# Seven-product units stored with their sums, and SBUF moved from GpSimd's descriptor room to buffers

## The chip, the cores and the metric

The kernel runs on one core of one Trainium2 chip. TensorE does the matrix products, VectorE (DVE), ScalarE (ACT) and GpSimd (POOL) the elementwise work, and SyncE (SP) issues most of the DMA transfers. The metric is the device time of one execution in microseconds (us). Of several runs the median is taken.

## The reference

Two layers of a decoder trunk, on 256 rows of 2048 columns in float32. The part around the change is the MLP:

```python
for l in range(DEPTH):                       # DEPTH = 2
    h = _rmsnorm(x, attn_norm_g[l])
    ...                                      # attention, gated convolution
    x = x + jnp.concatenate([attn, conv], axis=-1) @ w_out[l]
    hm = _rmsnorm(x, mlp_norm_g[l]) @ w_up[l]            # 2048 -> 8192
    x = x + jnp.square(jax.nn.relu(hm)) @ w_down[l]      # 8192 -> 2048
```

## The kernel before, in words

**Precision.** Every float32 operand is cut into two parts of type float32r, a high one (an ACT copy) and the rest (a VectorE subtraction). A product is then three matmuls: high by high, high by low, low by high. So each weight tile costs ACT and VectorE one instruction each (`halves`, lines 291 and 292; `column`, lines 719 and 720).

**The MLP of a layer** (`mlp`, from line 693) has a left and a right half.

*Left half.* A loop runs over 32 pairs of hidden blocks (a pair is 256 hidden columns). For pair i, `up_part` multiplies the normed activations (`nT`) with two columns of w_up, each in two passes `kh`; `evict` adds the two parts into a tile `h` of [128, 8, 128]; `square` applies relu, a scaling by the ratio of the two row tiles' norms (`mnorm.ratio`, made by the matmul at line 462), and the square. Planes 0 to 3 of `h` are the four 128x128 blocks A11, A21, A12, A22 of the pair: two row tiles by two hidden blocks. Planes 4 to 7 are sums S1 to S4 of them. `in_forms` makes these sums with four VectorE additions (lines 890 to 893) and cuts all eight planes into `f` (lines 895 and 896). Two pairs later (LAG) the pair's `f` meets the left 1024 columns of w_down in seven products instead of eight (Strassen's scheme), whose weight operands are four quarters and four sums of quarters (`quarters`: `b1`, `b2`, `t`, `t13`, `t24`, from a tile `draw`). Seven PSUM banks gather these products over the pairs. The last two pairs are multiplied plainly (line 985).

*Right half.* The same pairs meet the right 1024 columns of w_down. Twelve of them (SEVEN: 4, 6, 8, 11, ... 28) are again done with seven products, the twenty others (PLAIN) with eight (line 1060). What they need was stored in DRAM during the left half by GpSimd's DMA queue: of a plain pair the cut planes 0 to 3 (`plain`, line 883, two pairs to a tensor), of a unit the four squared planes in float32 (`hid`, line 879). In the right half `block(b)` loads two plain pairs in one transfer into a tile `g` (line 955, GpSimd's queue; the four tiles are shared with `nT`), and `load_again` loads a unit into a tile `h` (line 806, SyncE's queue); `unit` then runs `in_forms` on it, sums and cuts, and asks for the next unit. Matmuls of the right half write to banks named `rt`.

**Buffers.** `h` has one tile, `f` two; `draw` two; `uraw` (columns of w_up, and rows of w_down of plain pairs in the right half) three; `t24` one. GpSimd's DMA descriptors have 16384 bytes of each partition, the default.

**What sets the order.** TensorE's instructions run in program order. Those of the other engines and the DMA queues are ordered when the kernel is built, by a planner that simulates a time line; each engine then runs its own list in that order and waits where an operand or a buffer is missing. Weight cuts are listed as jobs: `weights.take()` makes them three ahead of use (AHEAD), in an order written out in `weights.order`, in which the four jobs of a unit (plain quarters, sums, the unit's `f`, further sums) stand between the rows of the plain pairs ahead of it. Small pieces of background work (`work.start`, `work.tick`) are put between the matmuls, a piece's `yield n` being n ticks; in `up_part` a tick stands after every four matmuls. `factors` is the piece that makes the row norms and, for the MLP, the ratio matmul.

**The first pair** (i = 0) runs its two columns side by side: both use one PSUM tile `up0` of two banks, in the order first pass of column 0, first pass of column 1, second pass of column 0 with its eviction, second pass of column 1 with its eviction.

## Time and profile before

| | us |
|---|---|
| three runs | 2167.89, 2167.99, 2170.19 |
| median | 2167.99 |
| profiled execution | 2165.76 |
| its span | 2164.0 |

The profile is of one execution. Its page gives busy times by engine, DMA queues, and the chain of work that ended last. By that chain 85% of the span is TensorE, 7% VectorE, 4% DMA. The mean granted clock of TensorE was 0.998. The stages in the span, by the chain: the mixer of layer 0 until about 395 us, its MLP until about 1090 us (right half from 912), the mixer of layer 1 until about 1469, its MLP to the end (right half from about 1985). In rows of the timeline the columns are start, duration, engine, line, operation, tiles and shapes, and in brackets the idle time before it with what ended it. A DMA row's time in the chain is from its issue to its landing.

### The profile page before, as it was taken

How to read it: one execution, taken by the hardware profiler on the slowest of the kernel's cores; microseconds unless marked ns; L12 is line 12 of the kernel's file. 1: busy time of each engine (PE TensorE's matmuls, PEld its weight loads, DVE VectorE, ACT ScalarE, POOL GpSimd, SP SyncE). 2: the span in 40 equal slices, each digit the busy share in tenths (PEclk: the TensorE clock that was granted, in tenths of full speed). 3: DMA queues.
4: the chain of work that ended last, by engine and by line, in shares of the span. 5: the costliest groups of instructions: out<-in, count | busy, mean ns of one | idle time of the engine just before them, and what ended most of it. 6: DMA issues, size and time to landing. Idle time of an engine off the chain costs nothing.

```text
span 2164.0 us, 29108 instructions
## 1 busy us (share of the span) xinstructions
PE 2136.1 (99%) x10966; PEld 1812.7 (84%) x10966; DVE 1710.8 (79%) x2397; ACT 1300.9 (60%) x1760; POOL 166.2 (8%) x246
## 2 busy tenths in 40 slices
PE   9999999999999999999999999999999999999999
PEld 7888888888888888788788888888888888887877
DVE  5677655698888888799866776557988888887997
ACT  6556445566666666656565664446666666665554
POOL 3021200000000000000001222000000000000000
PEclk9999999999999999999999999999999999999999
DMA  7655766587767777887565557656777767778873
GB/s 256 183 158 166 236 187 188 160 263 217 227 216 231 224 224 223 272 288 275 188 184 176 156 166 245 186 172 196 253 227 219 224 216 232 222 224 274 310 271 108
DMA packets 285534, 467.62 MB, mean 216 GB/s; under 512 B 10611, under 2 KB 191429, under 8 KB 282832
## 3 DMA queue, kind: packets, MB, share of 16 engines
q1 hardware_dynamic: 268128, 413.17, 61.2%
q0 software_dynamic: 17216, 52.56, 7.0%
q8 instruction: 86, 1.41, 0.3%
q14 instruction: 56, 0.46, 0.1%
q10 hardware_dynamic: 48, 0.02, 0.0%
HBM read 436.32 MB, written 29.38 MB: 215 GB/s over the span
## 4 chain that ended last, share of the span: by engine, by line
PE 85%; DVE 7%; DMA 4%; issue 2%; ACT 1%; POOL 1%; DVEq 0%; POOLq 0%; ACTq 0%
PE upc L856 30%; PE pr L904 13%; PE o L361 8%; PE rt L1060 5%; PE gb L383 4%; PE v L361 4%; PE ci L383 4%; PE gc L383 4%; PE rt L904 3%; PE q L361 3%; PE k L361 3%; DVE wlo L292 2%; DMA draw<-in_w_down_dram 1%; DMA h<-hid 1%; PE upw L856 1%
## 5 line engine op out<-in xcount | busy, mean ns | idle before, releaser
L291 ACT ACTIVATE whi<-raw 128x1024 fp32r<-128x1024 f32 (+1 forms) x338 | 355.6, 1054 | 410.6 <-PE rt L1060 87.8
L292 DVE TENSOR_TENSOR wlo<-raw,whi 128x1024 fp32r<-128x1024 f32 (+1 forms) x338 | 414.4, 1229 | 237.3 <-ACT whi L291 232.7
L856 PE MATMUL upc<-nT,uhi 128*128 128x512 f32 x1920 | 477.6, 391 | 0.0
L719 ACT ACTIVATE uhi<-uraw 128x1024 fp32r<-128x1024 f32 x256 | 271.2, 1060 | 288.1 <-PE upc L856 254.2
L856 PEld LDWEIGHTS upc<-nT,uhi 128*128 128x128 f32 x1920 | 352.8, 188 | 68.2
L720 DVE TENSOR_TENSOR ulo<-uraw,uhi 128x1024 fp32r<-128x1024 f32 x256 | 313.0, 1223 | 115.7 <-ACT uhi L719 113.3
L856 PEld LDWEIGHTS upc<-nT,ulo 128*128 128x128 f32 x1920 | 261.9, 190 | 18.7
L856 PE MATMUL upc<-nT,ulo 128*128 128x256 f32 x1920 | 267.7, 282 | 0.0
L1060 PE MATMUL rt<-whi,g 128*128 128x512 f32 x608 | 194.0, 393 | 0.0
L361 PE MATMUL o<-whi,cat 128*128 128x512 f32 x512 | 159.6, 390 | 0.0
L1060 PEld LDWEIGHTS rt<-whi,g 128*128 128x128 f32 x608 | 115.7, 190 | 24.1
L1060 PE MATMUL rt<-wlo,g 128*128 128x512 f32 x304 | 120.3, 396 | 9.4 <-DVE wlo L292 9.2
L361 PEld LDWEIGHTS o<-whi,cat 128*128 128x128 f32 x512 | 96.1, 188 | 19.7
L754 DVE TENSOR_TENSOR t<-draw 128x1024 f32<-128x1024 f32 x84 | 102.4, 1219 | 11.0 <-DMA draw<-in_w_down_dram 10.8
L740 ACT ACTIVATE b2h<-draw 128x1024 fp32r<-128x1024 f32 x84 | 88.9, 1058 | 34.6 <-PE pr L904 25.9
L896 DVE TENSOR_TENSOR f<-h,f 128x1024 fp32r<-128x1024 f32 (+1 forms) x88 | 105.2, 1196 | 0.2 <-ACT f L895 0.2
L741 DVE TENSOR_TENSOR t13l<-t,t13h 128x1024 fp32r<-128x1024 f32 x84 | 102.8, 1224 | 2.0 <-ACT t13h L740 0.5
L741 DVE TENSOR_TENSOR t24l<-t,t24h 128x1024 fp32r<-128x1024 f32 x84 | 102.4, 1219 | 0.6 <-ACT t24h L740 0.2
L741 DVE TENSOR_TENSOR b2l<-draw,b2h 128x1024 fp32r<-128x1024 f32 x84 | 102.4, 1219 | 0.4 <-ACT b2h L740 0.3
L361 PE MATMUL o<-wlo,cat 128*128 128x512 f32 x256 | 99.6, 389 | 0.0
L895 ACT ACTIVATE f<-h 128x1024 fp32r<-128x1024 f32 (+1 forms) x88 | 90.4, 1027 | 9.4 <-DVE h L893 9.2
L740 ACT ACTIVATE t24h<-t 128x1024 fp32r<-128x1024 f32 x84 | 88.4, 1052 | 9.6 <-DVE t L758 6.4
(359 smaller groups left out, 3841.9 us busy)
## 6 DMA issues: line engine op xcount, KB each, us to landing
uraw<-in_w_up_dram SPq DMA_DIRECT2D x128, 1024.0 KB, 6.5
raw<-in_w_in_dram SPq DMA_DIRECT2D x191, 512.0 KB, 4.0
draw<-in_w_down_dram SPq DMA_DIRECT2D x88, 1024.0 KB, 5.4
raw<-in_w_down_dram SPq DMA_DIRECT2D x40, 1024.0 KB, 5.6
raw<-in_w_out_dram SPq DMA_DIRECT2D x64, 512.0 KB, 3.6
plain<-f POOLq DMA_DIRECT2D x40, 512.0 KB, 6.5
g<-plain POOLq DMA_DIRECT2D x20, 1024.0 KB, 8.3
hid<-h POOLq DMA_DIRECT2D x24, 256.0 KB, 5.5
```

The source lines that it names most:

```text
L291: a = nc.scalar.activation(hi[:, k], raw[:, k], AF.Copy)
L292: d = nc.vector.tensor_sub(lo[:, k], raw[:, k], hi[:, k].bitcast(F32))
L361: nc.tensor.matmul(acc[:, t], a.ap[:, pa, k % KG, t * P:(t + 1) * P], (hi, lo)[pw][:, j], start=(k == 0 and n == 0), stop=(k == nk - 1 and ...
L383: nc.tensor.matmul(acc[:, f, 0] if part else acc[:, f], wt[:, k % 4, fs], a.ap[:, 0, k % KG] if part else a.ap[:, :, k % KG], start=(part ...
L719: nc.scalar.activation(hi, src, AF.Copy)
L720: nc.vector.tensor_sub(lo, src, hi.bitcast(F32))
L740: keep(nc.scalar.activation(hi, src, AF.Copy))
L741: keep(nc.vector.tensor_sub(lo, src, hi.bitcast(F32)))
L856: nc.tensor.matmul(acc[:, 0] if part else acc, wt[:, k], a.ap[:, 0, k % KG] if part else a.ap[:, :, k % KG], start=(part == 0 and kh == 0 ...
L896: nc.vector.tensor_sub(f[:, 1, :n], h[:, :n], f[:, 0, :n].bitcast(F32))
L904: nc.tensor.matmul(prods[n], f[:, pa, a], b[pw], start=(start and m == 0), stop=(stop and m == 2))
L1060: nc.tensor.matmul(prods[p], blocks[b][:, slot, pa, 2 * k + t], w[pw][:, n], start=(i == PLAIN[0] and k == 0 and m == 0), stop=False)
```

## The change

It does these things:

- The sums S1 to S4 of a unit are made before the pair is stored, and `hid` keeps seven planes (all but A21, which no product uses by itself) instead of four. In the right half a unit is only loaded and cut, seven planes wide (`rounded`), with no additions.
- So that the seven planes lie side by side, A11 and A21 change places, and A12 and A22: the roles of the two row tiles are exchanged, in the products' outputs too.
- `h` gets two tiles instead of one, `draw` three instead of two, `t24` two instead of one. GpSimd's descriptor room goes from 16384 to 4096 bytes per partition.
- A block is loaded in two transfers, one for each of its pairs. Block 1 and the first unit are asked for inside the right half's loop instead of ahead of it, the later blocks one plain pair later than before.
- The first pair's two columns get a PSUM tile each.
- The ratio matmul of the MLP's norm comes after nine ticks instead of five.

```diff
-                yield 5
+                yield 9
                 tp = bank("rbc")
...
-    A11, A21, A12, A22, S1, S2, S3, S4 = range(8)
+    A21, A11, A22, A12, S1, S2, S3, S4 = range(8)
...
-            dpool = scope.enter_context(tc.tile_pool(name="dpool", bufs=2))
+            dpool = scope.enter_context(tc.tile_pool(name="dpool", bufs=3))
...
-                    h, lw = parts(forms["t"][:, 2:4], "t24", 1)
+                    h, lw = parts(forms["t"][:, 2:4], "t24", 2)
...
-            hid = {i: dram.tile([P, 4 * P], F32, name=f"hid{l}_{i}") for i in SEVEN}
+            hid = {i: dram.tile([P, 7 * P], F32, name=f"hid{l}_{i}") for i in SEVEN}
...
             def load_again(i):
-                again[i] = fpool.tile([P, 8, P], F32, tag="h", name="h", bufs=1)
-                nc.sync.dma_start(again[i][:, :4].rearrange("p a c -> p (a c)"), hid[i])
+                again[i] = fpool.tile([P, 8, P], F32, tag="h", name="h", bufs=2)
+                nc.sync.dma_start(again[i][:, 1:].rearrange("p a c -> p (a c)"), hid[i])
...
-                    f = in_forms(again[i], True)
+                    f = rounded(again[i], 1, 8)
...
-                if i in hid:
-                    nc.gpsimd.dma_start(hid[i], u)
-                f = in_forms(h, i < NP - LAG)
...
+                if i < NP - LAG:
                     nc.vector.tensor_add(h[:, S1], h[:, A21], h[:, A22])
                     nc.vector.tensor_sub(h[:, S2], h[:, S1], h[:, A11])
                     nc.vector.tensor_sub(h[:, S3], h[:, A11], h[:, A21])
                     nc.vector.tensor_sub(h[:, S4], h[:, A12], h[:, S2])
+                if i in hid:
+                    nc.gpsimd.dma_start(hid[i], h[:, 1:].rearrange("p a c -> p (a c)"))
+                    return rounded(h, 1, 8)
+                f = rounded(h, 0, 8 if i < NP - LAG else 4)
+                b = PLAIN.index(i)
+                nc.gpsimd.dma_start(plain[b // 2][:, b % 2], f[:, :, :4])
+                return f
+
+            def rounded(h, lo, hi):
                 f = fpool.tile([P, 2, 8, P], F32R, tag="f", name="f")
-                nc.scalar.activation(f[:, 0, :n], h[:, :n], AF.Copy)
-                nc.vector.tensor_sub(f[:, 1, :n], h[:, :n], f[:, 0, :n].bitcast(F32))
+                nc.scalar.activation(f[:, 0, lo:hi], h[:, lo:hi], AF.Copy)
+                nc.vector.tensor_sub(f[:, 1, lo:hi], h[:, lo:hi], f[:, 0, lo:hi].bitcast(F32))
                 return f
...
-                h = fpool.tile([P, 8, P], F32, tag="h", name="h", bufs=1)
+                h = fpool.tile([P, 8, P], F32, tag="h", name="h", bufs=2)
                 if i == 0:
-                    two = mm.tile([P, 2, CH], F32, tag="mm2", name="up0")
-                    two = [two[:, c].rearrange("p (h s) -> p h s", h=2) for c in range(2)]
+                    two = [mm.tile([P, 2, CH], F32, tag="mm2", name=f"up{c}")[:, 0].rearrange(
+                        "p (h s) -> p h s", h=2) for c in range(2)]
...
             def block(b):
                 blocks[b] = apool.tile([P, 2, 2, 4, P], F32R, tag="a", name="g")
-                nc.gpsimd.dma_start(blocks[b], plain[b])
+                for s in range(2):
+                    nc.gpsimd.dma_start(blocks[b][:, s], plain[b][:, s])
 
             block(0)
-            block(1)
-            load_again(SEVEN[0])
...
-            OWN = ((0, 0, 2), (0, 1, 4), (1, 0, 3), (1, 1, 8))
-            left = [xs[n][:, t] for n in range(2) for t in range(NT)]
-            right = [xs[2 + n][:, t] for n in range(2) for t in range(NT)]
+            OWN = ((0, 1, 2), (0, 0, 4), (1, 1, 3), (1, 0, 8))
+            left = [xs[n][:, t] for n in range(2) for t in (1, 0)]
+            right = [xs[2 + n][:, t] for n in range(2) for t in (1, 0)]
...
-                if slot == 0 and b + 2 < len(plain):
+                if slot == 0 and b == 0:
+                    block(1)
+                if slot == 1 and b + 2 < len(plain):
                     block(b + 2)
+                if slot == 1 and b == 0:
+                    load_again(SEVEN[0])
...
-    nc = _bacc.Bacc("TRN2", target_bir_lowering=False, num_devices=1)
+    nc = _bacc.Bacc("TRN2", target_bir_lowering=False, num_devices=1,
+                    dynamic_dma_scratch_size=4096)
```

More of the change, by code (lines that the diff above doesn't have):

```diff
@@ L877, in square @@
                 nc.scalar.activation(u, u, AF.Square)
-                if i in hid:
-                    nc.gpsimd.dma_start(hid[i], u)
-                f = in_forms(h, i < NP - LAG)
-                if i not in hid:
-                    b = PLAIN.index(i)
-                    nc.gpsimd.dma_start(plain[b // 2][:, b % 2], f[:, :, :4])
-                return f
-            def in_forms(h, sums):
-                n = 4
-                if sums:
-                    n = 8
+                if i < NP - LAG:
                     nc.vector.tensor_add(h[:, S1], h[:, A21], h[:, A22])
```

## The prediction

> **What bounds the kernel now.** I read the page first, then sums over stretches of time, then the timeline of TensorE for every place where it sat idle, and last the chain of waits at those places. The page:

> ```profile
> span 2164.0 us, 29108 instructions
> PE 2136.1 (99%) x10966; PEld 1812.7 (84%) x10966; DVE 1710.8 (79%) x2397; ACT 1300.9 (60%) x1760; POOL 166.2 (8%) x246
> ```

> TensorE is busy for all but 28 us. The change alters no matmul count, so it can only take idle time away, or add some. Two stretches in the body of the MLP (us, then busy time of PE, PEld, DVE, ACT, POOL, then clock, DMA share, GB/s), the first from the columns of w_up, the second from the right half of w_down:

> ```profile
> 438.83:885.72 446.89, 446.42 (x2382) 385.64 (x2381) 399.25 (x539) 300.44 (x365) 18.97 (x29) 1.00 0.74 227
> 951.54:1022.94 71.40, 71.40 (x316) 59.14 (x316) 69.79 (x91) 45.74 (x48) 2.12 (x4) 1.00 0.79 275
> ```

> Both bodies are full. In the second VectorE has only 1.6 us to spare in 71.4 us, that is in seven periods of 10.2 us (one seven-product pair and one plain pair). So what there is to win lies at the borders. The timeline of TensorE, with the idle time and its releaser in brackets, shows these waits in the MLP of layer 0 (first six) and of layer 1 (last six):

> ```profile
> 402.44 0.46 PE L462 MATMUL rbc<-diag,ones 128*128 128x128 f32 x2 [0.53 <-DVE diag L459]
> 407.75 0.49 PE L856 MATMUL up<-nT,uhi 128*128 128x512 f32 x1 [1.57 <-ACT ev L866]
> 477.20 0.50 PE L904 MATMUL pr<-b1h,f 128*128 128x512 f32 x1 [0.47 <-DVE f L896]
> 914.38 0.50 PE L1060 MATMUL rt<-wlo,g 128*128 128x512 f32 x1 [1.62 <-DVE wlo L292]
> 920.25 0.50 PE L1060 MATMUL rt<-wlo,g 128*128 128x512 f32 x1 [2.81 <-DVE wlo L292]
> 1056.43 0.50 PE L904 MATMUL rt<-b1h,f 128*128 128x512 f32 x1 [1.76 <-DVE f L896]
> ...
> 1476.35 0.46 PE L462 MATMUL rbc<-diag,ones 128*128 128x128 f32 x2 [0.53 <-DVE diag L459]
> 1480.77 1.42 PE L856 MATMUL up<-nT,uhi 128*128 128x512 f32 x5 [0.69 <-ACT ev L866]
> 1549.69 0.50 PE L904 MATMUL pr<-b1h,f 128*128 128x512 f32 x1 [0.47 <-DVE f L896]
> 1987.23 0.50 PE L1060 MATMUL rt<-wlo,g 128*128 128x512 f32 x1 [1.98 <-DVE wlo L292]
> 1993.10 0.80 PE L1060 MATMUL rt<-wlo,g 128*128 128x512 f32 x1 [2.81 <-DVE wlo L292]
> 2092.99 0.50 PE L904 MATMUL rt<-b1h,f 128*128 128x512 f32 x1 [1.50 <-DVE f L896]
> ```

> They add up to 16.7 us. Nearly all of them are in code that the diff touches.

> **Part by part.**

> *The ratio matmul (yield 5 to 9).* It is put four ticks later, from inside the third of the four first column passes to its end. Its input is ready 0.53 us after TensorE now asks for it, and a tick is four matmuls, so the wait goes in both layers: 1.1 us. It moves past no DMA, and its reader, the scaling of the first pair, comes only after the second half is copied out.

> *Two PSUM tiles for the first pair.* Now both column halves share one tile, and the last pass of the second half waits until ACT has copied out the first: 1.57 and 0.69 us. With a tile each this wait is gone. What is late next? In layer 0 ACT stood before that copy at a weight cut, behind this load (chain of waits):

> ```profile
> 395.61 10.46 DMA uraw<-in_w_up_dram
> ```

> It landed at 406.07, and the passes that need those weights come after the second half's last pass, so they are covered. But TensorE now comes some 2 us earlier into the first products, where VectorE is behind. Bounds 0 and 2.3 us; I take 1.6, nearer the whole, since the cuts there are released by TensorE and move with it. The second tile takes the buffer of the last output projection, whose two additions the transposes ahead of it wait for anyway: nothing.

> *Two h tiles.* The first pairs' f comes 0.47 us late in both layers, since a pair's eviction waits until the f before it is made. Bounds 0 and 0.9 us, I take 0.6: VectorE is nearly full there.

> *The start of the right half.* This is the largest term. TensorE waits for wlo, and VectorE, which makes it, had itself waited (first the chain of waits, then GpSimd, SyncE and VectorE in the timeline):

> ```profile
> 898.23 13.72 DMA draw<-in_w_down_dram
> 1970.72 14.07 DMA draw<-in_w_down_dram
> ...
> 896.62 1.12 POOL L955 DMA_DIRECT2D g<-plain  x2 [5.05 <-PE upc L856]
> 899.41 1.06 POOL L955 DMA_DIRECT2D g<-plain  x2 [1.67 <-PE upc L856]
> 905.43 0.34 SPq L806 DMA_DIRECT2D h<-hid  x1
> 911.97 1.23 DVE L754 TENSOR_TENSOR t<-draw 128x1024 f32<-128x1024 f32 x1 [5.23 <-DMA draw<-in_w_down_dram]
> 1984.82 1.22 DVE L754 TENSOR_TENSOR t<-draw 128x1024 f32<-128x1024 f32 x1 [5.59 <-DMA draw<-in_w_down_dram]
> ```

> The weights of the first seven-product unit (pair 4) were issued only when one of the two draw tiles came free, and then shared the DMA engines with four blocks of 1 MB, hence 13.7 us. The sum t for unit 4 stands in VectorE's queue ahead of the wlo that TensorE needs, and all of it stands for 5.2 and 5.6 us. After the wait VectorE has a long row of work and TensorE stops twice.

> With three draw tiles this load need not wait for the rows of pair 30; it can go a tile earlier, some 10 us, before the blocks. Then VectorE's 5.2 us of waiting go, and the two stops in each layer, 4.4 and 4.8 us, lose nearly that. Where the blocks stand matters less: GpSimd issues them when a tile is free, not when TensorE gets to them, and I expect most of the four to start at the same time as before. The halved load lets the first pair start on half a block, but it is not what is waited for.

> The second stop carries another cost (stretches as above):

> ```profile
> 917.80:921.20 3.40, 0.95 (x4) 0.81 (x5) 3.40 (x5) 2.02 (x3) 0.00 (x0) 1.00 0.82 247
> 921.20:924.60 3.40, 3.40 (x10) 2.64 (x9) 3.40 (x6) 0.04 (x1) 0.00 (x0) 0.50 0.99 371
> 1993.00:1996.60 3.60, 3.50 (x9) 2.79 (x10) 3.60 (x8) 0.00 (x0) 0.00 (x0) 0.53 1.01 369
> ```

> After a stop of 2.81 us the granted clock is half for 3.4 us: half of that, about 1.5 us a layer with what overlaps at its ends, 3.0 in all. After the stops of 1.62 and 1.98 us it stays whole.

> Together 9.2 us of stops and 3.0 us of half clock, 12.2 us; bounds 0 and 12.2. I take 9.5: three quarters of the stops (6.9), because VectorE's row of work is still there and TensorE would come to it earlier, and of the slow clock 2.6, nearer the whole, since stops only a third shorter carry none.

> [...]

> *Sums kept with the unit.* In the right half each unit drops four additions and makes f of seven parts instead of eight. From the groups by line, VectorE between 951 and 1022 us, and from the chain of waits:

> ```profile
> L896 DVE TENSOR_TENSOR f<-h,f 128x1024 fp32r<-128x1024 f32 x6 | 7.3, 1220 | 0.2 <-ACT f L895 0.2
> L890 DVE TENSOR_TENSOR h<-h 128x128 f32<-128x128 f32 x7 | 2.0, 288 | 1.9 <-DMA h<-hid 1.9
> L893 DVE TENSOR_TENSOR h<-h 128x128 f32<-128x128 f32 x6 | 1.7, 286 | 0.0
> ...
> 1030.31 5.28 DMA h<-hid
> 1042.82 3.48 DMA h<-hid
> ```

> Four additions at 0.2 (start to start in a row) to 0.29 us, and an eighth of 1.22: 0.95 to 1.3 us less in each period. VectorE's 9.97 us of 10.2 (69.79 over 7) become about 9.0. The load of the next unit, today started only when f is made because there is one tile, gets a tile of its own and a period's lead. So the stops at 1056.43 and 2092.99, which end a long run of full VectorE and waits for h, should go: 3.26 us, of which I take 3.0 (bounds 0 and 3.26).

> In the first half the additions stay, but stand before the store. The store leaves about 1.1 us later; nothing reads it before the right half.

> *What is added.* The DMA issues (KB each, median us to landing):

> ```profile
> draw<-in_w_down_dram SPq DMA_DIRECT2D x88, 1024.0 KB, 5.4
> plain<-f POOLq DMA_DIRECT2D x40, 512.0 KB, 6.5
> g<-plain POOLq DMA_DIRECT2D x20, 1024.0 KB, 8.3
> hid<-h POOLq DMA_DIRECT2D x24, 256.0 KB, 5.5
> h<-hid SPq DMA_DIRECT2D x24, 256.0 KB, 3.7
> ```

> The unit grows from 256 to 448 KB, both ways; from these rows its load should take 4 to 6.5 us, under a lead of about ten. Its cost if the cover is gone is that difference, up to 2.8 us, once per unit. Twenty more GpSimd issues of about 0.55 us lie in an engine that is busy 8%. GpSimd's room: before the right half at most five of its transfers are under way. Even if it could keep only one, four blocks one after the other would take 33 us from 896, to 929, while the third is first needed behind the first unit (chain of waits):

> ```profile
> 941.34 4.76 PE rt L904 x21
> 946.10 5.44 PE rt L1060 x24
> ```

> So I cost the quarter room at nothing; below zero there is nothing to have. The exchange of A11 with A21 and A12 with A22 only renames planes and turns the order of output rows: nothing.

> *The sum.* 1.1 + 1.6 + 0.6 + 9.5 + 3.0 = 15.8 us. The profiled execution took 2165.76 us (span 2164.0), so 2150.0; the median of the three runs, 2167.99, stands 2.2 us above it, so I forecast **2152.2 us**.

> **Rivals.**

> *The wait only moves (to the unit's load, or to ACT's queue).* f of unit 4 is now ACT's first touch of the loaded tile, and that load, issued at 905.43, starts inside the block burst. If ACT's queue has it ahead of the weight cuts, they wait for the landing. The order of ACT, VectorE and the queues is made by a planner that already set t too early once, which speaks for it; the second h tile, which lets the load start before 905, speaks against. The start then gives perhaps 2 of its 9.5: gain 8.3, time about 2160.

> *New order, no change.* The planner's lists change everywhere, and small waits of the size of 0.5 to 1.6 us come up in the first columns and the start of the next mixer: 12 to 16 us of them would eat the gain. The full bodies above speak against so many. About 2168.

> *The DMA becomes the bound of the right half (slower).* A period moves 1024 + 448 + 1024 + 512 KB, 3.08 MB, in 10.2 us: 302 GB/s, where the stretch above shows 275 at a share of 0.79. In proportion that is a share of 0.87, and 371 GB/s were seen in a short stretch at 0.99, so there should be room. If landings lengthen so that only 275 are had, a period takes 11.2 us, and 24 of them cost 24 us against 15.8: about 2176. The point from which it is slower than before is 0.66 us per period, 284 GB/s. The three draw tiles and two h tiles are against it.

> **How the numbers follow.** Forecast 0.60, the moved wait 0.21, no change 0.09, DMA bound 0.10. The first two are faster, so 0.81 faster, 0.09 within 0.2% (4.3 us, about what a measurement of this kernel can tell from no change) and 0.10 slower. The forecast's own bounds: all terms whole are 19.8 us and some 1.2 us of pipeline filling behind the stops, so 2147; all at the taken values but the start at half, 2157. The range runs to 2147 below and, to hold the moved wait and a part of the third case, to 2166 above.

> **What would show it.** Right: no 0.53 us before the ratio matmul; no wait for ev before the last pass of the first pair; the draw load of unit 4 issued before 895 us and VectorE not idle at t of unit 4; no half clock near 921; VectorE near 9.0 us per period and no stop for f at the end of the units. Wrong: ACT or VectorE idle for h<-hid at the start of the right half; DMA share over 0.95 in its body with landings of draw over 10 us; GpSimd's issues longer than about 1 us.

## The result and the profile after

| | before | after |
|---|---|---|
| median of ten runs each, us | 2168.00 | 2163.75 |
| lowest to highest | 2166.08 to 2171.34 | 2161.19 to 2166.62 |
| profiled execution | 2165.76 | 2163.51 |
| its span | 2164.0 | 2161.7 |

The ratio after to before is 0.9980, 95% interval 0.9972 to 0.9988. The kernel became faster by 4.3 us, where 15.8 were forecast. The forecast range holds the time; its size is wrong.

The page of the changed kernel, the rows that answer to the first ones of before, and the same stretch of the right half:

```profile
span 2161.7 us, 29004 instructions
...
PE 2136.9 (99%) x10966; PEld 1815.0 (84%) x10966; DVE 1692.1 (78%) x2301; ACT 1301.1 (60%) x1760; POOL 176.1 (8%) x266
...
951.54:1022.94 71.40, 71.40 (x317) 59.12 (x316) 66.67 (x67) 45.51 (x49) 4.24 (x8) 1.00 0.86 297
```

VectorE runs 96 instructions less (24 units by four additions) and is busy 18.7 us less, 0.78 us per unit. The right half does move more, 297 GB/s at a share of 0.86, close to the 302 and 0.87 of the prediction. So the parts do what they were said to do, though VectorE is relieved by less than the 0.95 to 1.3 us per unit that were forecast (9.5 us per period in this stretch, 66.67 over 7, where about 9.0 were forecast). Where TensorE waits is another matter (its timeline, the waits over 0.4 us in the MLP; layer 0, then layer 1):

```profile
404.26 0.95 PE L856 MATMUL up<-nT,uhi 128*128 128x512 f32 x3 [0.75 <-DVE nT L256]
430.58 0.50 PE L902 MATMUL pr<-t13l,f 128*128 128x512 f32 x1 [2.38 <-DVE t13l L741]
908.43 0.50 PE L982 MATMUL pr<-whi,f 128*128 128x512 f32 x1 [1.49 <-ACT f L893]
911.43 1.22 PE L982 MATMUL pr<-whi,f 128*128 128x512 f32 x2 [2.26 <-DVE f L894]
...
1474.93 0.98 PE L856 MATMUL up<-nT,uhi 128*128 128x512 f32 x3 [0.75 <-DVE nT L256]
1500.59 0.50 PE L902 MATMUL pr<-t13l,f 128*128 128x512 f32 x1 [1.67 <-DVE t13l L741]
1980.84 0.80 PE L982 MATMUL pr<-whi,f 128*128 128x512 f32 x1 [3.89 <-ACT f L893]
1983.83 1.22 PE L982 MATMUL pr<-whi,f 128*128 128x512 f32 x2 [1.77 <-DVE f L894]
```

Every wait that the prediction listed is gone (the ratio, ev, the first f, wlo, the late f), and eight new ones stand in their place, together 15.0 us where there were 16.7. The largest four are no longer in the right half but just ahead of it, in the plain products of the last two pairs (line 982). Their releaser is `f` of pair 31. Why it is late shows in the timeline of ScalarE:

```profile
904.23 0.63 ACT L740 ACTIVATE b1h<-draw 128x512 fp32r<-128x512 f32 x1 [2.42 <-DMA draw<-in_w_down_dram]
904.77 0.61 ACT L873 ACTIVATE h<-h 128x512 f32<-128x512 f32 x1
905.29 1.04 ACT L291 ACTIVATE whi<-draw 128x1024 fp32r<-128x1024 f32 x1
907.09 0.63 ACT L877 ACTIVATE h<-h 128x512 f32<-128x512 f32 x1 [0.76 <-DVE h L875]
907.75 0.63 ACT L893 ACTIVATE f<-h 128x512 fp32r<-128x512 f32 x1
...
1976.63 0.63 ACT L740 ACTIVATE b1h<-draw 128x512 fp32r<-128x512 f32 x1 [4.83 <-DMA draw<-in_w_down_dram]
```

The cut `b1h` of the *second* unit of the right half (pair 6) stands in ACT's list ahead of the relu, the square and the `f` of pair 31, and waits for its weights. Those loads, in the chain of waits, were issued at 895.58 and 1965.99:

```profile
895.58 8.62 DMA draw<-in_w_down_dram
...
1965.99 10.62 DMA draw<-in_w_down_dram
```

As forecast, the first unit's load came early: SyncE issues the 33rd draw load of the layer, unit 4's, at 880.37 instead of 898.23. That left the place behind it to unit 6's load, and the planner gave unit 6's cut the place that unit 4's had had.

The stretches around these stops (us, busy time of PE, PEld, DVE, ACT, POOL, then clock, DMA share, GB/s) show DMA engines that are full (a packet counts where it starts, so a share can pass 1), and half the clock behind the stops in both layers, for 3.4 us in layer 0 and 10.2 in layer 1, together twice the 6.8 us of before:

```profile
906.55:911.40 4.85, 1.13 (x4) 0.30 (x2) 4.85 (x9) 3.05 (x4) 0.00 (x0) 0.99 1.13 413
911.40:914.80 3.40, 3.37 (x8) 2.70 (x9) 3.28 (x4) 1.06 (x1) 0.72 (x1) 0.51 1.14 410
...
1979.70:1989.94 10.24, 7.33 (x16) 5.35 (x17) 8.04 (x10) 4.95 (x6) 0.71 (x1) 0.50 1.00 330
```

**Where the time went by stage.** A matmul's start in TensorE's timeline marks each border. For layer 0 of the changed kernel:

```profile
395.74 0.84 PE L856 MATMUL up<-nT,uhi 128*128 128x512 f32 x3
425.75 0.40 PE L902 MATMUL pr<-b1h,f 128*128 128x512 f32 x1
898.32 1.12 PE L856 MATMUL upc<-nT,ulo 128*128 128x256 f32 x8
918.11 0.39 PE L1061 MATMUL rt<-whi,g 128*128 128x512 f32 x1
1086.31 0.39 PE L1046 MATMUL rt<-whi,g 128*128 128x512 f32 x1
```

First columns: from the first `up` to the first `pr` (30.01 us here). Products: to the last `upc` (the eighth of the third row, 899.15). Plain end: to the first `rt`. Right half: to the last `rt`. Both layers added, for all kernels of this study, with their medians (taken at different times, so compare the ratios given below, not medians a few us apart). The stages are those of one profiled execution, which can stand some us off the median: e5's is the fastest of five (2147.04), e10's the slowest of eleven (2172.42).

| kernel | first columns | products | plain end | right half | the last two | median |
|---|---|---|---|---|---|---|
| before | 62.4 | 943.3 | 26.1 | 352.1 | 378.2 | 2168.0 |
| after | 60.1 | 946.1 | 41.6 | 333.9 | 375.5 | 2163.75 |
| e1 | 60.0 | 940.9 | 35.1 | 337.3 | 372.4 | 2156.51 |
| e2 | 60.1 | 947.4 | 26.5 | 338.2 | 364.7 | 2154.13 |
| e3 | 60.1 | 949.8 | 38.6 | 333.9 | 372.5 | 2167.02 |
| e4 | 60.0 | 953.7 | 26.5 | 337.4 | 363.8 | 2159.37 |
| e5 | 60.1 | 941.1 | 26.1 | 337.0 | 363.2 | 2151.35 |
| e6 | 60.1 | 942.1 | 26.1 | 340.1 | 366.2 | 2150.43 |
| e7 | 60.0 | 948.8 | 26.1 | 336.5 | 362.6 | 2154.47 |
| e8 | 60.1 | 941.1 | 26.1 | 337.0 | 363.2 | 2148.80 |
| e9 | 62.9 | 943.0 | 26.1 | 349.8 | 376.0 | 2163.99 |
| e10 | 65.1 | 943.9 | 42.5 | 336.3 | 378.7 | 2169.62 |
| e11 | 60.1 | 944.5 | 26.1 | 353.9 | 380.0 | 2167.29 |
| e12 | 59.6 | 941.1 | 26.1 | 338.2 | 364.3 | 2145.91 |
| e13 | 60.1 | 944.3 | 26.1 | 347.5 | 373.7 | 2161.93 |
| e14 | 60.1 | 941.2 | 26.1 | 334.7 | 360.9 | 2144.00 |
| e15 | 59.5 | 941.0 | 26.1 | 336.8 | 362.9 | 2147.23 |

The changed kernel wins 18.2 us in the right half, more than the 12.5 forecast there, and gives 15.5 of them back in the 26 us ahead of it, and 2.8 in the products.

### The profile page after: what moved, and what is told of

Same layout as the page of the kernel before. It is cut to its first block, busy times and chain, and to the rows that moved or that the text cites. A ratio compares the mean times of both kernels' runs of the same rounds, so it can differ in the third digit from the quotient of the medians.

```text
span 2161.7 us, 29004 instructions
## 1 busy us (share of the span) xinstructions
PE 2136.9 (99%) x10966; PEld 1815.0 (84%) x10966; DVE 1692.1 (78%) x2301; ACT 1301.1 (60%) x1760; POOL 176.1 (8%) x266
## 4 chain that ended last, share of the span: by engine, by line
PE 92%; DVE 3%; DMA 2%; issue 2%; POOL 1%; ACT 1%; DVEq 0%; POOLq 0%; ACTq 0%
PE upc L856 30%; PE pr L902 13%; PE rt L1061 10%; PE o L361 8%; PE rt L902 5%; PE ci L383 4%; PE gc L383 4%; PE gb L383 4%; PE v L361 4%; PE q L361 3%; PE k L361 3%; DMA draw<-in_w_down_dram 1%; PE up L856 1%; PE pr L982 1%; DVE ulo L720 1%
## 5 line engine op out<-in xcount | busy, mean ns | idle before, releaser
L292 DVE TENSOR_TENSOR wlo<-raw,whi 128x1024 fp32r<-128x1024 f32 (+1 forms) x338 | 414.6, 1229 | 273.7 <-ACT whi L291 267.8
L856 PE MATMUL upc<-nT,uhi 128*128 128x512 f32 x1920 | 477.6, 391 | 0.0
L856 PEld LDWEIGHTS upc<-nT,uhi 128*128 128x128 f32 x1920 | 352.7, 188 | 68.3
L856 PEld LDWEIGHTS upc<-nT,ulo 128*128 128x128 f32 x1920 | 261.9, 190 | 18.7
L856 PE MATMUL upc<-nT,ulo 128*128 128x256 f32 x1920 | 267.7, 282 | 0.0
L361 PEld LDWEIGHTS o<-whi,cat 128*128 128x128 f32 x512 | 96.1, 188 | 19.8
L754 DVE TENSOR_TENSOR t<-draw 128x1024 f32<-128x1024 f32 x84 | 102.3, 1218 | 0.6 <-DMA draw<-in_w_down_dram 0.6
L894 DVE TENSOR_TENSOR f<-h,f 128x896 fp32r<-128x896 f32 (+2 forms) x88 | 98.7, 1121 | 0.2
L902 PE MATMUL pr<-t13h,f 128*128 128x512 f32 x240 | 93.8, 391 | 0.0
L740 ACT ACTIVATE t13h<-t 128x1024 fp32r<-128x1024 f32 x84 | 89.4, 1064 | 6.4 <-PE rt L902 2.4
## 6 DMA issues: line engine op xcount, KB each, us to landing
uraw<-in_w_up_dram SPq DMA_DIRECT2D x128, 1024.0 KB, 5.9
raw<-in_w_in_dram SPq DMA_DIRECT2D x191, 512.0 KB, 4.0
draw<-in_w_down_dram SPq DMA_DIRECT2D x88, 1024.0 KB, 5.9
raw<-in_w_down_dram SPq DMA_DIRECT2D x40, 1024.0 KB, 6.4
raw<-in_w_out_dram SPq DMA_DIRECT2D x64, 512.0 KB, 3.7
plain<-f POOLq DMA_DIRECT2D x40, 512.0 KB, 3.8
g<-plain POOLq DMA_DIRECT2D x40, 512.0 KB, 9.6
```

The lines of the kernel that those rows point to most:

```text
L292: d = nc.vector.tensor_sub(lo[:, k], raw[:, k], hi[:, k].bitcast(F32))
L361: nc.tensor.matmul(acc[:, t], a.ap[:, pa, k % KG, t * P:(t + 1) * P], (hi, lo)[pw][:, j], start=(k == 0 and n == 0), stop=(k == nk - 1 and ...
L740: keep(nc.scalar.activation(hi, src, AF.Copy))
L754: keep(nc.vector.tensor_sub(t[:, 0:2], raw[:, :, 1], raw[:, 0]))
L856: nc.tensor.matmul(acc[:, 0] if part else acc, wt[:, k], a.ap[:, 0, k % KG] if part else a.ap[:, :, k % KG], start=(part == 0 and kh == 0 ...
L902: nc.tensor.matmul(prods[n], f[:, pa, a], b[pw], start=(start and m == 0), stop=(stop and m == 2))
```

## The experiments

Two theories. **The place**: the loss at the border goes where a cut stands in an engine's list ahead of `f`, behind a load that has not landed; a third draw tile moves this to the next unit, and fills a transfer in at the layer's start besides. **The load**: the DMA engines are too full there (a share of 1.13 in the stretch above), so that something waits wherever it stands. The function `late` of the program forbids the planner to move an instruction ahead of its place in the program's text; "held" below means that. Of a unit, its cuts and sums on ACT and VectorE are held, for its right columns; the loads stay free. Where an expectation speaks of held weight loads, or in e9 of left columns, these cuts and sums are meant. Line numbers are those of each kernel.

**e1: two draw tiles.** The changed kernel with

```diff
-tc.tile_pool(name="dpool", bufs=3)
+tc.tile_pool(name="dpool", bufs=2)
```

> The changed kernel with two draw tiles again instead of three, all else as changed. Theory A (third tile): the third tile lets weight loads start a unit earlier; the planner then puts the first cuts of unit 6 ahead of the last steps of pair 31, and at the layer's start a third load of 1 MB takes bandwidth from the columns of w_up. So without it the waits of the plain products (L982, with the half clock after them 14.8 us in both layers) and most of the wait for t13l at the first products (some 4 of 5.0 us) go, and the waits at the first plain pair of the right half come back, 10 to 13 us: about 2155 to 2159 us. Theory B (transfers): the unit of 448 KB and the blocks in halves lengthen every landing at the start of the right half; then the waits at L982 stay with two tiles as well, about 2163 us or more.

2156.51 us, ratio 0.9942 (0.9928 to 0.9956). The time lies in theory A's range, but in part by luck: the stops ahead of the right half did not go (2.83 and 2.71 us at line 982), and at the first plain pairs only 0.91 and 0.89 us came. The stop at the layer's start (`t13l`) is gone, so the third tile made it. At the border it is now unit 4 again, in VectorE's timeline, and TensorE stops for the `f` behind it:

```profile
905.97 1.23 DVE L754 TENSOR_TENSOR t<-draw 128x1024 f32<-128x1024 f32 x1 [3.69 <-DMA draw<-in_w_down_dram]
907.12 0.68 DVE L894 TENSOR_TENSOR f<-h,f 128x512 fp32r<-128x512 f32 x1
```

**e2: unit 6 held.** The changed kernel with the cuts of the right columns of unit 6 held:

```diff
-keep = late if i == 0 and col == 0 else lambda ins: None
+keep = late if (i, col) in ((0, 0), (SEVEN[1], 2 * CH)) else lambda ins: None
```

> The changed kernel with the first two weight jobs of unit 6 (quarters and sums, cuts on ACT and VectorE) pinned behind all that is written ahead of them on their engine, so that they can't stand ahead of pair 31's relu, square and f. Three draw tiles stay. Theory A: the waits at L982 and the half clock go, 14.8 us, and nothing else comes late: about 2149 us (2147 to 2153). Theory B: the landings are as late as before, so a wait of several us appears at the first plain pairs or the first unit: 2158 to 2164 us.

2154.13 us, ratio 0.9929 (0.9912 to 0.9945), about 1 us above theory A's range. One condition takes the plain end from 41.6 to 26.5 us; the right half gives 4.3 of these 15 back. The loads are no earlier (the two behind one another are issued from 896.48 on, 895.58 in the changed kernel), and the DMA engines are nearly as full as there (a share of 1.09 against 1.13). Yet TensorE works all through the stretch in which it stood in the changed kernel (columns as above), so the place is what matters:

```profile
906.55:911.40 4.85, 4.85 (x22) 3.78 (x21) 3.57 (x4) 2.72 (x3) 0.71 (x1) 1.00 1.09 378
```

**e3 and e4: the third tile filled later.** The load of the layer's third draw tile held (e3), and both holds (e4):

```diff
-nc.sync.dma_start(
+a = nc.sync.dma_start(
...
+if i == 2 and col == 0:
+    late(a)
```

> The changed kernel with the left-half load of pair 2's weights pinned on SyncE's queue behind all loads written ahead of it, so that the third draw tile isn't filled before the columns of w_up that the first pairs need. Theory A: the wait for t13l at the first products falls from 2.4 and 1.7 us to 0.1 to 0.3: about 4 us less, 2160 us. Theory B: the wait has another cause (TensorE comes there 2 us earlier, VectorE is behind anyway): 2162 to 2164 us.

> Both pins together. Theory A: the two gains add, about 18 us: 2145 us (2143 to 2149). Theory B: 2158 us or more.

2167.02 us, ratio 0.9991 (0.9981 to 1.0002), and 2159.37 us, 0.9956 (0.9941 to 0.9970). Theory A misses in both; e4 lies in theory B's range, e3 above it. The stop for `t13l` goes, but the held load comes out together with the next one, and ACT waits for the two (e3; ACT, then TensorE):

```profile
448.27 0.63 ACT L742 ACTIVATE b1h<-draw 128x512 fp32r<-128x512 f32 x1 [3.89 <-DMA draw<-in_w_down_dram]
...
455.17 2.11 PE L858 MATMUL upc<-nT,uhi 128*128 128x512 f32 x8 [2.23 <-ACT ev L868]
1527.55 3.78 PE L858 MATMUL upc<-nT,uhi 128*128 128x512 f32 x8 [3.56 <-ACT ev L868]
```

This is the same fault at another place: two loads of 1 MB at once, and a cut that stands ahead of an eviction.

**e5: two tiles, units 4 and 6 held** (e1's edit, and `(SEVEN[0], 2 * CH)` added to e2's list).

> The changed kernel with two draw tiles and with the first two weight jobs of units 4 and 6 pinned behind all that is written ahead of them on their engine. Theory A (now: what is lost at the start of the right half is the planner's place for the units' cuts, whichever unit's load is under way; the third tile itself is not needed): the waits of the plain products in the run with two tiles, 2.98 and 2.86 us and the half clock behind them (1.3 to 1.5 us each), go, and part of the 1.0 us at the first plain pairs: 2146 to 2150 us. Theory C (without the third tile the load of unit 4 comes too late wherever its cuts stand): the wait moves to the first plain pairs or to the first unit, 3 us or more a layer: 2153 to 2158 us.

2151.35 us, ratio 0.9919 (0.9905 to 0.9934), about 1 us above theory A's range. In the profiled execution TensorE's timeline has these waits left over 0.4 us in layer 0's MLP (0.75 and 0.82 us in layer 1); the clock is 1.00 from 395 to 450, from 930 to 1060 and from 2000 to 2100 us, and 0.999 on the mean of the execution:

```profile
404.50 0.96 PE L856 MATMUL up<-nT,uhi 128*128 128x512 f32 x3 [0.75 <-DVE nT L256]
921.68 0.50 PE L1061 MATMUL rt<-wlo,g 128*128 128x512 f32 x1 [0.49 <-DVE wlo L292]
```

Unit 4's load is issued at 895.77, 14.1 us ahead of the right half's first matmul, just as in the kernel before (898.23 and 912.37); it lands after 10.5 us instead of 13.7. The stop at the border went without an early load and without a third tile. The rival theory of the full DMA engines falls, as e2 has shown and e9 shows again with a load as slow as before.

**e6, e7, e13: the unit's two parts.** On top of e5: the four sums made again on loading, `hid` with four planes (e6); one `h` tile (e7); both (e13).

```diff
-hid = {i: dram.tile([P, 7 * P], F32, name=f"hid{l}_{i}") for i in SEVEN}
+hid = {i: dram.tile([P, 4 * P], F32, name=f"hid{l}_{i}") for i in SEVEN}
...
-again[i] = fpool.tile([P, 8, P], F32, tag="h", name="h", bufs=2)
+again[i] = fpool.tile([P, 8, P], F32, tag="h", name="h", bufs=1)
```

> The kernel of e5 with the units stored as four planes again (256 KB) and the four sums made again by VectorE when a unit is loaded; two h tiles and the cut of seven planes stay. If the dropped additions are what removed the stops for f late in the right half (VectorE full: 9.97 of 10.2 us per period before), VectorE is near 9.9 us per period again, and the stops of 1.5 to 1.8 us come back: about 3 us more than e5. If the second h tile removed them, the same time as e5 within 1 us.

> The kernel of e5 with one h tile, seven planes stored and no additions in the right half. If the second h tile is what removed the stops for f, they come back (late units: 1.5 to 1.8 us a layer; first products: 0.5 us a layer), about 4 us more than e5. If the dropped additions alone removed the late ones, only the 0.5 us at the first products come back: about 1 us more.

> The kernel with two draw tiles and three held weight loads (2151 us), with both one h tile and the sums made again on loading: the unit is as in the kernel before. Theory that one of the two is enough for the late units but without both the stops for f come back: 2154.5 (one h tile) plus about 3.3 us late in the right half and some at the first units, 2158 to 2161 us. Theory that the unit's parts do nothing in the right half: 2154 to 2156, as with one h tile alone.

2150.43 us, 0.9921 (0.9906 to 0.9937); 2154.47 us, 0.9936 (0.9923 to 0.9950); 2161.93 us, 0.9971 (0.9959 to 0.9982). By the ratios e6 costs 0.4 us and e7 3.7 against e5, both within the intervals, and the two together 11. Neither alone brings the late stops for `f` back: e7's time is that of the theory of the second `h` tile, but what it loses stands in the left half (948.8 us of products against 941.1), and e6's right half is 3.1 us longer in the profile without such a stop. With both the right half takes 347.5 us, nearly as long as that of the kernel before with the same units held (e9, 349.8). The stops are back, for `f` of the units (e13, TensorE):

```profile
1015.82 0.50 PE L907 MATMUL rt<-b1h,f 128*128 128x512 f32 x1 [2.04 <-ACT f L898]
1017.85 0.50 PE L907 MATMUL rt<-b1h,f 128*128 128x512 f32 x1 [1.29 <-DVE f L899]
2055.35 0.50 PE L907 MATMUL rt<-b1h,f 128*128 128x512 f32 x1 [1.44 <-DVE f L899]
2089.24 0.50 PE L907 MATMUL rt<-b1h,f 128*128 128x512 f32 x1 [1.56 <-DVE f L899]
```

With a second `h` tile and the sums made again VectorE is as full as before (e6 first, then e5, the same stretch):

```profile
951.54:1022.94 71.40, 71.03 (x314) 58.50 (x313) 69.21 (x93) 44.01 (x48) 4.24 (x8) 1.00 0.82 278
...
951.54:1022.94 71.40, 71.40 (x317) 59.12 (x316) 66.32 (x69) 43.65 (x49) 4.24 (x8) 1.00 0.88 310
```

What the second tile spares it are waits for a unit that has not landed. The table of waits of VectorE, 920 to 1080 us, for e13 and for e6 (us in total, times, longest; in layer 1, from 1985 to 2140 us, the two differ less, 5.1 and 3.7 us); in e5 and e7, where no addition stands in VectorE's list behind the load, there is no such row:

```profile
DVE h L811 <- DMA h<-hid: 6.9, 4, 4.4
...
DVE h L811 <- DMA h<-hid: 1.0, 1, 1.0
```

**e9: the kernel before, units 4 and 6 held**, nothing else.

> The kernel before, with nothing changed but the planner's place for the weight loads of units 4 and 6 (left columns of the pair's first and third rows), each held where its step stands in the program. The load of unit 4 still waits for one of two draw tiles and shares the DMA engines with four whole blocks. Theory that the place in the planner's lists is the larger part: the two waits for wlo in each layer (4.4 and 4.8 us) and most of the half clock behind them (3.0 us) go, while the stops at 407.75 (1.57 and 0.69 us), the two for f late in the right half (3.3 us), 0.47 and 0.53 us a layer stay: 2168 less 9 to 12, so 2156 to 2159 us. Theory that the load itself comes too late as long as the blocks are asked for first and the tiles are as they were: no gain, 2164 to 2168 us.

2163.99 us, ratio 0.9981 (0.9970 to 0.9991): neither 2156 to 2159 nor nothing. The waits for `wlo` are gone, though unit 4's load is as late and as slow as before: issued at 899.08, again 14.1 us ahead of the first matmul of the right half, it takes 13.7 us (first row; KB and us to landing). The right half is only 2.3 us shorter, since TensorE now stops for `f` or `t24` further on (second row, and at 1021.40, 2022.72 and 2024.58), with a clock of 0.50 behind the first of these, from 1005.55 to 1012.00. Ahead of the first, VectorE had waited 2.06 and 1.35 us for a unit (`h<-hid`) in its one tile:

```profile
draw<-in_w_down_dram SPq DMA_DIRECT2D x1, 1024.0 KB, 13.7
...
1005.55 0.80 PE L904 MATMUL rt<-b1h,f 128*128 128x512 f32 x1 [2.73 <-ACT f L895]
```

**e10: the kernel before with a third draw tile**, nothing else.

> The kernel before with a third draw tile and nothing else. The prediction held that this alone lets the load of unit 4 go a tile earlier and takes the start of the right half away: 2168 less 9.5, about 2158 us. The theory from the trace of after: the third tile is filled at the layer's start and delays the w_up columns there (about 2 us more at the first products of each layer), and at the start of the right half the planner sets the next unit's cut as early as it had set unit 4's, so that the stops stay at another place: 2164 to 2170 us.

2169.62 us, ratio 1.0009 (0.9999 to 1.0018). The load of unit 4 goes at 884.14, and the waits stand in the plain end (2.46 and 2.76 us in layer 0, 1.84 and 3.25 in layer 1, all for `f`). Plain end and right half together take 378.7 us against 378.2 of before.

**e11: the first pair alone.** The kernel before with the ratio matmul at nine ticks and two PSUM tiles for the first pair.

> The kernel before with the ratio matmul nine ticks down and a PSUM tile for each column of the first pair, and nothing else. Prediction: 1.1 + 1.6 us, so about 2165 us. The theory from the trace of after: the ratio's 0.53 us a layer come back as 0.75 us a layer before nT, the wait for ev (1.57 and 0.69 us) goes, and without a third draw tile nothing new comes at the first products: 2165 to 2167 us. The two differ in the trace alone: a wait for nT of 0.75 us ahead of the second pass or none.

2167.29 us, ratio 1.0003 (0.9994 to 1.0012); the 2.7 us of the prediction would be 0.9988, outside this interval. In the profiled execution the first columns are 2.3 us shorter, as in the changed kernel, but products and right half grow by 3.0; small waits for `t13l`, for the first `f` and for `wlo` grew. `nT` is waited for 0.75 us in each layer.

**e12: the ratio back at five ticks** (e5 with `yield 5`).

> The kernel with two draw tiles and the three weight loads held at their places (the one that measured 2151 us), with the ratio matmul back at five ticks. Theory: the 0.53 us wait for the ratio comes back and stands in the time of the 0.75 us wait for nT, which goes or shrinks: within 1 us of 2151. If the nine ticks are worth the 1.1 us of the prediction, 2152.5.

2145.91 us, ratio 0.9906 (0.9892 to 0.9919), against e5's 0.9919 (0.9905 to 0.9934). The median is 5 us below the 2151 near which both theories put it; the intervals overlap, so no gain of five ticks is shown. The trace carries the smaller statement: 0.53 us for the ratio stand in place of 0.75 for `nT`, and the first columns are 0.5 us shorter. Nine ticks are worth nothing.

**e8, e15: descriptor room.** e5 with the full room and one `t24` tile (e8), and that with five ticks (e15).

```diff
-h, lw = parts(forms["t"][:, 2:4], "t24", 2)
+h, lw = parts(forms["t"][:, 2:4], "t24", 1)
...
-                    dynamic_dma_scratch_size=4096)
+                    )
```

> The kernel of e5 with GpSimd's descriptor room at its default of 16384 bytes again (and one t24 tile instead of two, for the space). The prediction costs the quarter room at nothing: the same time as e5 within 2 us. If GpSimd waits for room now, its issues of blocks and stores are earlier here and the time is lower by more than that.

> The kernel with two draw tiles and three held weight loads, the ratio matmul at five ticks, one t24 tile and GpSimd's full descriptor room: the two edits that measured 2145.9 and 2148.8 us taken together. Theory that neither the room nor the second t24 tile does anything: 2145 to 2149 us. If the second t24 tile has a share, stops for t24l of 0.5 us come up in the right half and it is 2150 or more.

2148.80 us, 0.9909 (0.9893 to 0.9925); 2147.23 us, 0.9902 (0.9886 to 0.9918). The median of e8 is 2.6 us below that of e5, where 2 were allowed, but the intervals overlap those of e5 and e12, and the stages are the same to 0.1 us (e8 against e5). Room and `t24` tile do nothing that can be measured.

**e14: the blocks as before** (e5, but each block in one transfer, blocks 0 and 1 and the first unit asked for ahead of the right half's loop).

> The kernel with two draw tiles and three held weight loads (2151 us), with the blocks loaded whole, block 1 and the first unit asked for ahead of the right half's loop and the later blocks one plain pair earlier, all as in the kernel before. Prediction: where the blocks stand matters little, so 2151 us within 1.5 us. Rival, that four whole blocks at once ahead of the draw load of unit 4 are what made it late: the draw load lands after 12 us and the waits for wlo at the start of the right half return, 2155 to 2160 us.

2144.00 us, ratio 0.9889 (0.9873 to 0.9905), the fastest kernel of the study and below both expectations. The rival had one half right: unit 4's load takes 12.7 us, where e5's takes 10.5. But its cut is held, so nothing waits behind it. The right half is 2.3 us shorter than e5's, and the waits for `wlo` at its start (0.49 and 0.82 us) are gone. Later and halved blocks bring nothing; they cost 2.3 us by the profile and 6.5 by the ratios, whose intervals just touch, so the size is open.

## Why the prediction was wrong

The direction and the parts that leave were right: no wait for the ratio, ev, the first `f`, `wlo` or the late `f`, unit 4's load before 895, GpSimd's issues at about 0.54 us (four half blocks in 2.18), DMA share 0.86. Term by term:

*The start of the right half, 9.5 us: the step that failed.* It reads: "With three draw tiles this load need not wait ... Then VectorE's 5.2 us of waiting go, and the two stops in each layer ... lose nearly that." The load went earlier and VectorE's wait for unit 4 went, but the stops of 9.2 us became stops of 9.4 (1.49, 2.26, 3.89 and 1.77), with twice as long at half clock behind them. The plain end grew by 15.5 us, more than the 12.2 that these stops had cost, so the term is a loss of some 3 us where a gain of 9.5 was forecast. Its slow clock rested on "stops only a third shorter carry none", but shorter ones do (1.85 us in e10, 2.38 in e2). The step took the late load for the cause. The cause is that the planner puts a unit's cut ahead of work that TensorE needs sooner; a tile more shifts that by one unit (e10: nothing won). Holding the cut takes these stops away (e2, e5, e9), with the load issued as late as before; in e9 it also lands as late. The prediction had this as its rival "The wait only moves", for the unit's load or ACT's queue; it was right in kind, at 0.21, and wrong in the load that it named and in its price.

*The cost at the layer's start was missing.* The third draw tile also is filled there, ahead of columns of w_up, which the prediction costed at nothing because it looked at the tile only at the border. ACT's timeline after, where an `uraw` column is waited for:

```profile
417.07 1.06 ACT L719 ACTIVATE uhi<-uraw 128x1024 fp32r<-128x1024 f32 x1 [4.46 <-DMA uraw<-in_w_up_dram]
```

This column's load takes 16.1 us, where it took 13.0 in the kernel before and takes 12.7 in e1. It makes TensorE wait 2.38 and 1.67 us for `t13l`; e1 takes both away. So the first pair's 1.6 us (2.26 us of waits for ev did go, 4.05 came) became a loss of 1.8. e11 shows that even without this tile its gain does not show in the time; by its one profile it is given back in small waits behind it.

*The ratio, 1.1 us:* became −0.4 (two waits of 0.75 for two of 0.53). `nT` of the same norm is not ready either, and nothing in the prediction asked what TensorE would reach next.

*Two h tiles, 0.6:* 0.9, both waits of 0.47 gone. *Sums kept, 3.0:* 3.3, both late stops gone. These two were right in this sum, though VectorE's relief was smaller than forecast (0.78 us per unit). But as a pair they are worth more, about 11 us once the border is in order (e5 against e13), and either part alone keeps the late stops away (e6, e7).

*One cause behind two terms.* The table shows it as two by two, all with two draw tiles. Plain end and right half take 378.2 us (before), 376.0 (e9, held), 372.4 (e1, units relieved, which differs from the kernel before in the smaller parts too) and 363.2 (e5, both): 2.2 and 5.8 us alone, 15.0 together. With three draw tiles relief alone gives 375.5 (after), both 364.7 (e2). In the kernel before VectorE is behind, being nearly full and waiting for its units besides (`h<-hid`, 5.2 us from 920 to 1080 and 5.8 from 1985 to 2140); where TensorE waits for it, at the border, in the plain pairs or at a later unit, changes little. The prediction added "start" and "late stops" as two independent terms, though it saw VectorE with 1.6 us to spare in 71.4.

The other rivals: the DMA did not become the bound (TensorE busy for 71.40 of 71.40 us at a share of 0.86), and GpSimd's quarter room cost nothing, as forecast. The 1.2 us of "pipeline filling" in the range's lower bound were the author's estimate; the trace of before shows 0.11 us at such a stop (the matmul at 914.38 is followed by the next after 0.34 us, those further on in its row after 0.23). What stays open: why e14's earlier blocks help (its draw load of unit 4 is issued at 895.01, as in e5), and the products of e7, 7.7 us longer than e5's, of which its trace explains some four (a wait for ev of 2.60 us in layer 1, two of 0.47 for the first `f`, and a mean clock of 0.998 where e5 had 0.999).

## What to carry to other kernels

When an engine stands at a load, look first at what stands behind that instruction on its engine, and move the instruction; an earlier load or another buffer hands the place to the next load. Where several stops go back to one engine that is behind, they are one term: removing one moves most of the time to the next, and only relief and order together paid in full here. Look at a new buffer at every place where it is filled, not at the one where it is wanted.

## What was not expected of the hardware

In these traces the length of a stop does not by itself tell whether half clock follows. After a stop of 2.38 us the changed kernel goes on at full clock, and e2, after a stop of the same length at the same place of layer 1, does not (stretches of 3.4 us behind the stop; the clock is the third number from the end):

```profile
430.58:434.00 3.42, 3.42 (x19) 3.00 (x20) 3.42 (x6) 0.93 (x2) 0.00 (x0) 1.00 0.96 312
...
1498.03:1501.40 3.37, 3.37 (x10) 2.66 (x11) 3.37 (x6) 0.91 (x2) 0.00 (x0) 0.63 0.97 309
```

```profile
426.64:430.05 3.41, 1.57 (x7) 0.94 (x6) 3.41 (x5) 3.35 (x6) 0.00 (x0) 1.00 0.25 70
430.05:433.46 3.41, 2.88 (x14) 2.46 (x15) 3.41 (x6) 1.46 (x2) 0.00 (x0) 1.00 0.94 288
...
1495.49:1498.90 3.41, 1.03 (x5) 0.74 (x5) 3.41 (x5) 2.76 (x5) 0.00 (x0) 1.00 0.63 159
1498.90:1502.31 3.41, 3.41 (x11) 2.73 (x10) 3.41 (x6) 0.96 (x2) 0.00 (x0) 0.50 1.00 333
```

In the traces of before and after, from 60 us to 8 us ahead of the end, four stretches of the grid at full clock have TensorE idle for 2.45 to 2.77 us, and half clock follows on each; seven have it idle for 1.00 to 1.84 us, and it follows on none. The stop of 1.98 us in the kernel before, which a border cuts into 0.93 and 1.05 us, is not followed by it. In e2 2.38 us within one stretch were followed by half clock, and in e10 a stop of 1.85 us (at 410.86): the eight matmuls behind it took 3.41 us, where eight of the same form take 2.00. So in these traces the start of half clock goes with the idle time within one stretch of 3.413 us, not with the length of the whole stop.
